# Retention's values in two chunks of 512 columns, with the rotary key's 64 columns as matmuls of their own

## The chip, the core and the metric

The kernel runs on one core of a Trainium2 chip. The metric is the device time of one execution in microseconds. Three runs of the kernel before gave 816.58, 816.60 and 817.53 us; their median, 816.6 us, is the time to which the changed kernel is compared.

## What is computed

The reference is a trunk of two layers over 256 tokens of 2048 features, in float32. The first layer has a combined input projection, two groups of heads (retention and latent attention), a gate and an output projection; the second is a gated convolution module. What matters here is the input projection of the first layer:

```python
h = rms_norm(x, norm_g)
proj = h @ w_in
rq, rk, rv, cq, ckv, krope, gate = jnp.split(proj, list(SPLIT_A), axis=-1)
rv = rv.reshape(B, S, N_RET_HEADS, RET_HEAD_DIM)
k_rope = jnp.broadcast_to(krope[:, :, None, :], (B, S, N_MLA_HEADS, MLA_ROPE_DIM))
```

`rv`, the values of retention, is 1024 columns wide (8 heads of 128), and `krope`, the rotary part of the attention key that all heads share, is 64 columns wide. Both are the same input multiplied by different columns of one weight matrix, over a contraction of 2048.

## The kernel before

**Split products.** Every large product is made of three float32r matmuls (`mm3`, lines 193 to 195): an operand is split into a high part, rounded to float32r, and a low part, the remainder; high times high, high times low and low times high are summed in PSUM. Each of the three instructions loads its own stationary operand (128x128) into the array, also where two that follow one another have the same one.

**The weight stream.** Weights come from HBM through a class `Stream`, in units of 128 partitions by 2048 columns as a rule. A unit is loaded into a buffer `raw` (three of them) by a DMA on SP's queue (line 152). Each half of a unit is then split: ScalarE writes the high part `whi` (line 167, five buffers), and VectorE subtracts it to give the low part `wlo` (line 88 through the helper `tt`, four buffers). When the program asks for half j, the low parts up to half j+3 and the high parts up to half j+4 are issued first (`half`, lines 180 to 186), so that TensorE has some halves in hand. The order of the instructions on TensorE, ScalarE and VectorE is the order in which the program issues them.

**The clock of the program.** Each call of `half` also moves a program clock on to the next whole number and issues the small steps that are due by then (`tick`, `later`). `tick(True)` moves it by one half in between. So what ScalarE and VectorE do beside the weight stream is bound to the count of halves, not to time.

**The stages around the change.** First come the latents for the query (`kgroup`, with 256 tokens as moving columns) and for key and value (two calls of `pair`, also 256 moving columns). Then comes the stage of the values, lines 503 to 520: four chunks `c` of 272 columns, which are the 1024 columns of `rv` and the 64 of `krope` set side by side (1088 in all). Here the input is the stationary operand, 128 tokens at a time (`t` is 0 or 1), and the weights are the moving one. A chunk is 16 steps `k` of the contraction, by 2 token blocks, by the three matmuls of `mm3`: 96 matmuls of 272 columns. The four chunks are 384 of them, and use 8 units of 2176 columns, thus 16 halves of 1088 columns, of which each feeds 24 matmuls. Each chunk fills two PSUM banks (`mmps`, a ring of four) that ScalarE reads out with the norm's scale `Rt` into `vret` (line 518); the last chunk's columns 208 to 271 go to `krope` (line 520).

**What hangs on the stage.** While it runs, VectorE and ScalarE also normalise the latents and make the angles of the rotary embedding, bound to the program clock; TensorE makes two small sums over partitions for that (`token_cols`, line 315). Right behind the stage stand the squares and the rotation of `krope` on ScalarE and VectorE (lines 522 to 529), and then the heads, each with a `pair` (256 moving columns). From the heads on, `chunk` (lines 365 to 382) makes products with 512 moving columns: 16 steps by 2 token blocks by 3, that is 96 matmuls.

Of the kernel before, what the change touches and what calls it, by code (L numbers as in the profile page):

```python
# [10 lines left out]
AF = mybir.ActivationFunctionType  # L11
# [4 lines left out]
P = 128  # L16
T = 256
D = 2048
KT = D // P
# [3 lines left out]
ROPE = 64  # L23
# [3 lines left out]
RVC = 272  # L27
# [21 lines left out]
def body(ctx, tc, a):  # L49
    nc = tc.nc  # L50
    act = nc.scalar.activation
    V = nc.vector
# [12 lines left out]
    def nm(s):  # L65
        uid[0] += 1
        return f"{s}_{uid[0]}"

    def slot(i, dt=F32):
        return spool.tile([P, 2048], dt, tag=f"s{i}", name=nm(f"s{i}"))  # L70
# [7 lines left out]
    def mmps():  # L78
        return psm.tile([P, 512], F32, tag="mm", name=nm("mm"))
# [108 lines left out]
    st = Stream()  # L188

    def mm3(ps, l, r, start, stop):  # L190
        (lh, ll), (rh, rl) = l, r
        mm = nc.tensor.matmul
        mm(ps, lh, rh, start=start, stop=False, skip_group_check=True)  # L193
        mm(ps, lh, rl, start=False, stop=False, skip_group_check=True)  # L194
        mm(ps, ll, rh, start=False, stop=stop, skip_group_check=True)  # L195
# [17 lines left out]

    u_cq = [st.add(a["w_first"][u], V) for u in range(8)]
    u_ckv = [st.add(a["w_in"][i], V) for i in range(4)]
    u_rv = [[st.add(a["w_rv"][2 * c + h], V) for h in range(2)] for c in range(4)]
    u_qk, u_b = {}, {}
    for h in range(HEADS):
        u_qk[h] = [st.add(a["w_in"][4 + 2 * h + i], V) for i in range(2)]
# [28 lines left out]
    def kk(tiles, k):  # L248
        return tiles[k // 8][:, (k % 8) * T:(k % 8 + 1) * T]
# [6 lines left out]
    def consts(what):  # L256
        if what == 0:
            nc.sync.dma_start(posi[:, 0:T + 2], a["pos"])
            nc.sync.dma_start(cb[:, 0:CB_1], a["cb"][:, 0:CB_1])
        elif what == 1:  # L260
            nc.sync.dma_start(dmask[:, :], a["dmask"])
        elif what == 2:
            nc.sync.dma_start(ident[:, :], a["ident"])
            nc.sync.dma_start(amask[:, :], a["amask"])
        else:
            nc.sync.dma_start(cb[:, CB_1:CB_N], a["cb"][:, CB_1:CB_N])
# [8 lines left out]
    for q in range(1, 8):  # L275
        st.before[u_cq[q]] = [lambda q=q: x_load(q)]
    st.before[u_ckv[0]] = [lambda: consts(0)]
    st.before[u_rv[2][0]] = [lambda: consts(1)]
    st.before[u_rv[3][0]] = [lambda: consts(2)]
    st.before[u_rv[3][1]] = [lambda: consts(3)]  # L280

    def x_split(q):
        st.dma_to(q)
# [10 lines left out]
    Rt = cpool.tile([P, 2], F32, name="Rt")  # L294
# [89 lines left out]
    def xrhs(k):  # L384
        return kk(xh, k), kk(xl, k)
# [6 lines left out]
    krope = e0[:, 1024:1152].rearrange("p (t d) -> p t d", t=2)  # L392
# [108 lines left out]
    latent(ckv, 1)  # L501

    vret = slot(9)
    for c in range(4):
        pst = [mmps(), mmps()]
        for uh in range(2):
            for h in range(2):
                hi, lo = st.half(u_rv[c][uh], h)
                for i in range(4):
                    k = uh * 8 + h * 4 + i  # L510
                    w = slice(i * RVC, (i + 1) * RVC)
                    rh, rl = xrhs(k)
                    for t in range(2):
                        tk = slice(t * P, (t + 1) * P)
                        mm3(pst[t][:, :RVC], (rh[:, tk], rl[:, tk]), (hi[:, w], lo[:, w]), k == 0, k == KT - 1)
        for t in range(2):
            n = RVC if c < 3 else 208
            act(vret[:, t * 1024 + c * RVC:t * 1024 + c * RVC + n], pst[t][:, 0:n], AF.Copy, scale=Rt[:, t:t + 1])
            if c == 3:
                act(krope[:, t, :], pst[t][:, 208:272], AF.Copy, scale=Rt[:, t:t + 1])  # L520

    ksq = cpool.tile([P, 2], F32, name="ksq")
    for t in range(2):
# [164 lines left out]
    for h in range(HEADS):  # L688
        m1 = ret_rope(h, pair(u_qk[h], xrhs))
        later(4, lambda h=h, m1=m1: ret_scores(h, m1))  # L690
        if h < 3:
            pst = bproj(u_b[h], 0)
# [5 lines left out]
        elif h < 7:  # L698
            pst = bproj(u_b[h], 1024)
# [113 lines left out]
    for j in range(8):  # L813
        o = (j % 4) * 512
        ps = pair(u_gate[2 * j:2 * j + 2], xrhs)
# [49 lines left out]
    for c in range(4):  # L865
        ps = chunk(u_out[4 * c:4 * c + 4], mrhs)
# [286 lines left out]
    for c in range(4):  # L1153
        ps = chunk(u_cg[4 * c:4 * c + 4], yrhs)
# [26 lines left out]
    for k in range(KT):  # L1181
        hi, lo = st.half(u_co1[k // 2], k % 2)
        l = zrhs(k)
        for t in range(2):
            for c in range(2):
                w = slice(c * 512, (c + 1) * 512)
# [5 lines left out]
    for c in range(2):  # L1192
        us = u_co2[4 * c:4 * c + 4]
        if c == 0:
            ps = chunk(us, zrhs)
# [6 lines left out]
def layout(i):  # L1202
    import numpy as np
    f = np.float32
    A = lambda n: np.asarray(i[n])
    o = {}

    def feat(v):
        return v.reshape(-1, P).T

    def duo(w):
        k, n = w.shape
        return np.ascontiguousarray(w.reshape(2, k // P // 2, P, n // 256, 256).transpose(3, 0, 2, 1, 4)).reshape(n // P, P, -1)

    def kmaj(w, nk):
        k, n = w.shape
        return np.ascontiguousarray(w.reshape(k // P // nk, nk, P, n).transpose(0, 2, 1, 3)).reshape(k // P // nk, P, nk * n)

    def chunks(w, c):
        k, n = w.shape  # L1220
        return np.ascontiguousarray(w.reshape(k // P, P, n // c, c).transpose(2, 1, 0, 3))

    def wide(w):
        k, n = w.shape
        return np.ascontiguousarray(w.reshape(4, 4, P, n // 512, 512).transpose(3, 0, 2, 1, 4)).reshape(n // 128, P, 2048)

    x = A("x")[0]
    o["xt"] = x.reshape(2, P, D).transpose(1, 0, 2).reshape(P, -1)
    o["x"] = np.ascontiguousarray(x.T.reshape(KT, P, T).transpose(1, 0, 2)).reshape(P, -1)
    pos = A("positions")[0]  # L1230
    o["pos"] = np.concatenate([np.broadcast_to(pos[None, :], (P, T)), pos.reshape(2, P).T], 1)
    w = A("a_w_in")[0]
    rq, rk, rv, cq, ckv, kr, gate = np.split(w, [1024, 2048, 3072, 3584, 4096, 4160], axis=1)
    o["w_first"] = kmaj(cq, 2)
    qk = np.stack([rq.reshape(D, HEADS, P), rk.reshape(D, HEADS, P)], 2).reshape(D, -1)
    o["w_in"] = duo(np.concatenate([ckv, qk, gate], 1))
    o["w_rv"] = chunks(np.concatenate([rv, kr], 1), RVC).reshape(4, P, 2, -1).transpose(0, 2, 1, 3).reshape(8, P, -1)
    qb = A("a_w_q_b")[0].reshape(512, HEADS, QK)
    qb = np.concatenate([qb[:, :, :NOPE].reshape(512, -1), qb[:, :, NOPE:].reshape(512, -1)], 1)
    o["w_qb"] = chunks(qb, 512).reshape(3, P, -1)  # L1240
    kvb = A("a_w_kv_b")[0].reshape(512, HEADS, 2 * P)
    kvb = np.concatenate([kvb[:, :, :P].reshape(512, -1), kvb[:, :, P:].reshape(512, -1)], 1)
    o["w_kvb"] = chunks(kvb, 512).reshape(4, P, -1)
    o["w_out"] = wide(A("a_w_out")[0])
    cw = A("c_w_in")[0]
    ca_, cb_, cg_ = np.split(cw, 3, axis=1)
    ab = np.stack([ca_.reshape(D, 8, T), cb_.reshape(D, 8, T)], 2).reshape(D, -1)
    o["c_in"] = wide(np.concatenate([ab, cg_], 1))
    co = A("c_w_out")[0]
    o["c_out1"] = kmaj(co[:, :1024], 2)  # L1250
    o["c_out2"] = wide(co[:, 1024:])

    def inv(d):
        e = -np.arange(0, d, 2, dtype=f) / f(d)
        return np.power(10000.0, e.astype(np.float64)).astype(f)

    def rows(v):
        return np.broadcast_to(v[None, :], (P, v.shape[0]))

    i128 = inv(P)  # L1260
    sgn = np.concatenate([np.ones(64, f), -np.ones(64, f)])
    o["ca"] = np.concatenate([feat(A("a_norm_g")[0]), np.concatenate([i128, i128])[:, None], sgn[:, None], rows(inv(64))], 1)
    qn, kn = A("a_q_norm_g")[0], A("a_k_norm_g")[0]
    cwt = A("c_conv_w")[0].T.reshape(KT, P, TAPS).transpose(1, 0, 2).reshape(P, -1)
    o["cb"] = np.concatenate([feat(A("a_q_a_norm_g")[0]), feat(A("a_kv_a_norm_g")[0]), feat(A("a_ret_norm_g")[0]),
                              qn[:P, None], kn[:P, None], feat(A("c_norm_g")[0]), feat(A("c_conv_b")[0]),
                              feat(A("c_ln_g")[0]), feat(A("c_ln_b")[0]), rows(qn[P:]), rows(kn[P:]), cwt], 1)
    o["ident"] = np.eye(P, dtype=f)
    tri = np.where(np.arange(P)[None, :] <= np.arange(P)[:, None], 0.0, -1e30).astype(f)
    o["amask"] = np.concatenate([np.zeros((P, P), f), tri], 1)  # L1270
    lg = np.log1p(-(2.0 ** (-5.0 - np.arange(HEADS))))
    rel = (np.arange(T)[None, :] - np.arange(P)[:, None]).astype(np.float64)
    dm = np.where(rel >= 0, np.exp(lg[:, None, None] * np.maximum(rel, 0.0)[None]), 0.0) * P ** -0.5
    o["dmask"] = dm.transpose(1, 0, 2).reshape(P, -1).astype(f)
    return {k: np.ascontiguousarray(v) for k, v in o.items()}
# [22 lines left out]
```

## Time and profile before

| what | value |
|---|---|
| median of 3 runs | 816.6 us (816.58 to 817.53) |
| the profiled execution's own time | 816.11 us |
| its span in the trace | 814.3 us |
| instructions in the span | 12383 |
| TensorE matmul busy | 808.1 us (99%) |
| TensorE weight load busy | 720.7 us (89%) |
| VectorE busy | 594.8 us (73%) |
| ScalarE busy | 434.4 us (53%) |
| GpSimd busy | 221.8 us (27%) |
| granted TensorE clock | 1.0 |

The span is the time between the first and the last instruction that the profiler recorded, and the profiled execution took 1.8 us more than that. Busy times are shares of the span by engine. In the profile PE is TensorE's matmul, PEld its weight load, which runs beside it, DVE is VectorE, ACT is ScalarE and SP the engine that issues the DMAs. The recorded duration of one matmul is longer than the distance to the next, since matmuls are pipelined and their ends are modelled; what a matmul costs in a stream is the distance from its start to the next one's. A line such as `mm<-whi,s` names the output and the inputs by the program's names, `x96` is a count, and a bracket at the end of a row of the timeline is the idle time of the engine before that row with what ended it.

### The profile page before, as it was taken

The numbers are of one execution on the slowest core, as the hardware profiler recorded it, in microseconds if no ns is written. First come the engines' busy times: TensorE is split into PE (matmuls) and PEld (weight loads), VectorE is DVE, ScalarE is ACT, GpSimd is POOL, SyncE is SP. The second block draws the span as 40 slices with busy tenths as digits, with TensorE's granted clock in tenths as the row PEclk, the third lists the DMA queues.
The fourth block names the chain that finished last, engine by engine and source line by source line (L and its number), as shares of the span: only waits on it lengthen the run. The fifth ranks groups of instructions, "written<-read, shape, count | busy, mean of one in ns | idle before, by whom it ended". The sixth has DMA issues, their size and how long they took to land.

```text
span 814.3 us, 12383 instructions
## 1 busy us (share of the span) xinstructions
PE 808.1 (99%) x4766; PEld 720.7 (89%) x4766; DVE 594.8 (73%) x1093; ACT 434.4 (53%) x621; POOL 221.8 (27%) x127
## 2 busy tenths in 40 slices
PE   8999999999999999999999999999999999999998
PEld 8999999999999999998888888888888888888886
DVE  5878565699668755575555519999999999698542
ACT  6766544537445654664455644555544565676431
POOL 0000000000000000000000088899999999400000
PEclk9999999999999999999999999999999999999999
DMA  8974545526444443555545455455554554455650
GB/s 280 344 254 166 182 156 196 192 97 213 157 155 148 164 156 111 199 208 207 207 165 197 177 185 200 166 181 206 182 203 162 203 204 163 160 214 194 252 184 26
DMA packets 24106, 150.93 MB, mean 185 GB/s; under 512 B 2800, under 2 KB 3952, under 8 KB 6896
## 3 DMA queue, kind: packets, MB, share of 16 engines
q1 hardware_dynamic: 23616, 148.03, 51.0%
q0 software_dynamic: 288, 2.10, 0.6%
q8 instruction: 37, 0.61, 0.3%
q14 instruction: 21, 0.17, 0.1%
q10 hardware_dynamic: 144, 0.03, 0.0%
HBM read 148.04 MB, written 2.10 MB: 184 GB/s over the span
## 4 chain that ended last, share of the span: by engine, by line
PE 95%; DVE 2%; DMA 1%; ACT 1%; issue 0%; SPq 0%; DVEq 0%; ACTq 0%
PE mm L195 28%; PE mm L193 28%; PE mm L194 28%; PE aux L194 2%; PE aux L193 2%; PE aux L195 2%; DMA raw<-in_w_first 1%; DVE wlo L88 1%; DVE s L88 0%; PE mm L1108 0%; PE aux L853 0%; PE mm L1142 0%; PE aux L661 0%; PE aux L759 0%; PE aux L727 0%; PE aux L728 0%
## 5 line engine op out<-in xcount | busy, mean ns | idle before, releaser
L167 ACT ACTIVATE whi<-raw 128x1024 fp32r<-128x1024 f32 (+2 forms) x278 | 286.8, 1038 | 267.4 <-PE mm L195 177.3
L88 DVE TENSOR_TENSOR wlo<-raw,whi 128x1024 fp32r<-128x1024 f32 (+2 forms) x194 | 228.2, 1185 | 105.9 <-PE mm L194 51.8
L193 PE MATMUL mm<-whi,s 128*128 128x512 f32 (+1 forms) x760 | 285.2, 375 | 0.0
L195 PE MATMUL mm<-whi,s 128*128 128x512 f32 (+1 forms) x760 | 283.1, 372 | 0.0
L194 PE MATMUL mm<-wlo,s 128*128 128x512 f32 (+1 forms) x760 | 283.0, 372 | 0.0
L88 POOL TENSOR_TENSOR wlo<-raw,whi 128x1024 fp32r<-128x1024 f32 x84 | 201.5, 2411 | 33.6 <-PE mm L194 19.2
L91 DVE SCALAR_TENSOR_TENSOR aux<-s,cb,aux 128x256 f32<-128x256 f32 x480 | 190.0, 488 | 12.6 <-ACT aux L904 12.6
L193 PE MATMUL mm<-s,whi 128*128 128x256 f32 x636 | 183.4, 288 | 0.8 <-ACT whi L167 0.8
L195 PE MATMUL mm<-s,wlo 128*128 128x256 f32 x636 | 180.3, 284 | 0.6 <-DVE wlo L88 0.6
L194 PE MATMUL mm<-s,whi 128*128 128x256 f32 x636 | 179.8, 283 | 0.0
L195 PEld LDWEIGHTS mm<-whi,s 128*128 128x128 f32 x760 | 142.7, 188 | 25.0
L193 PEld LDWEIGHTS mm<-whi,s 128*128 128x128 f32 x760 | 142.9, 188 | 23.7
L194 PEld LDWEIGHTS mm<-wlo,s 128*128 128x128 f32 x760 | 142.8, 188 | 23.7
L193 PEld LDWEIGHTS mm<-s,whi 128*128 128x128 f32 x636 | 121.8, 192 | 1.6 <-ACT whi L167 1.0
L195 PEld LDWEIGHTS mm<-s,wlo 128*128 128x128 f32 x636 | 121.8, 191 | 1.4 <-DVE wlo L88 1.2
L194 PEld LDWEIGHTS mm<-s,whi 128*128 128x128 f32 x636 | 121.9, 192 | 0.6
L711 POOL MEMSET s<- 64x256 f32 x8 | 2.9, 361 | 232.3 <-PE mm L195 162.7
L890 POOL MEMSET s<- 128x30 f32 x16 | 1.1, 121 | 116.8 <-PE mm L194 101.0
L791 POOL DMA_DIRECT2D s<-in_xt x2 | 1.2, 618 | 97.2 <-PE aux L728 96.8
L193 PE MATMUL aux<-whi,s 128*128 128x512 f32 x64 | 25.0, 390 | 0.0
L195 PE MATMUL aux<-whi,s 128*128 128x512 f32 x64 | 24.9, 389 | 0.0
L194 PE MATMUL aux<-wlo,s 128*128 128x512 f32 x64 | 24.9, 389 | 0.0
(186 smaller groups left out, 550.1 us busy)
## 6 DMA issues: line engine op xcount, KB each, us to landing
raw<-in_c_in SPq DMA_DIRECT2D x48, 1024.0 KB, 4.8
raw<-in_w_in SPq DMA_DIRECT2D x36, 1024.0 KB, 4.8
raw<-in_w_out SPq DMA_DIRECT2D x16, 1024.0 KB, 4.8
raw<-in_c_out SPq DMA_DIRECT2D x16, 1024.0 KB, 4.8
raw<-in_w_rv SPq DMA_DIRECT2D x8, 1088.0 KB, 5.0
raw<-in_w_kvb SPq DMA_DIRECT2D x4, 1024.0 KB, 4.8
raw<-in_w_first SPq DMA_DIRECT2D x7, 512.0 KB, 4.9
raw<-in_w_qb SPq DMA_DIRECT2D x3, 1024.0 KB, 4.8
```

Of the source, the lines that this page charges most:

```text
L88: (eng or V).tensor_tensor(out=out, in0=in0, in1=in1, op=op)
L91: V.scalar_tensor_tensor(out=out, in0=in0, scalar=s, in1=in1, op0=op0, op1=op1)
L167: act(hi[:, :], self.raw[u][:, h * n:(h + 1) * n], AF.Copy)
L193: mm(ps, lh, rh, start=start, stop=False, skip_group_check=True)
L194: mm(ps, lh, rl, start=False, stop=False, skip_group_check=True)
L195: mm(ps, ll, rh, start=False, stop=stop, skip_group_check=True)
L711: G.memset(krz(i)[64 * b:64 * b + 64, :], 0.0)
L791: G.dma_start(x1[i][:, :], a["xt"][:, i * 2048:(i + 1) * 2048])
L890: G.memset(upad(c, 0, TAPS - 1), 0.0)
```

## The change

The columns of `rv` and of `krope` are no longer set side by side. `rv` is made by two calls of `chunk`, with 512 moving columns each: 192 matmuls of 512 columns instead of 384 of 272. `krope` becomes a product of its own: for 16 steps and 2 token blocks three matmuls with 64 moving columns, 96 in all, into one PSUM bank. The moving columns that pass through TensorE are the same in sum, 104448. The count of matmuls, each with its weight load, goes from 384 to 288. The unit of weights that is loaded for `krope` has 1024 columns, so its two halves have 512 columns and feed 48 matmuls each; the units of `rv` have 2048 columns, and their halves of 1024 feed 12 matmuls each. The stream gets one more unit (9 in place of 8), and the program clock advances by two more. The three loads of constants that stood ahead of the fifth, seventh and eighth unit of the stage stand ahead of the same ones. The readout by ScalarE is four instructions of 512 columns and two of 64, in place of six of 272, two of 208 and two of 64.

```diff
-    u_rv = [[st.add(a["w_rv"][2 * c + h], V) for h in range(2)] for c in range(4)]
+    u_rv = [[st.add(a["w_rv"][4 * c + h], V) for h in range(4)] for c in range(2)]
+    u_kr = st.add(a["w_kr"], V)
...
-    st.before[u_rv[2][0]] = [lambda: consts(1)]
-    st.before[u_rv[3][0]] = [lambda: consts(2)]
-    st.before[u_rv[3][1]] = [lambda: consts(3)]
+    st.before[u_rv[1][0]] = [lambda: consts(1)]
+    st.before[u_rv[1][2]] = [lambda: consts(2)]
+    st.before[u_rv[1][3]] = [lambda: consts(3)]
...
     vret = slot(9)
-    for c in range(4):
-        pst = [mmps(), mmps()]
-        for uh in range(2):
-            for h in range(2):
-                hi, lo = st.half(u_rv[c][uh], h)
-                for i in range(4):
-                    k = uh * 8 + h * 4 + i
-                    w = slice(i * RVC, (i + 1) * RVC)
-                    rh, rl = xrhs(k)
-                    for t in range(2):
-                        tk = slice(t * P, (t + 1) * P)
-                        mm3(pst[t][:, :RVC], (rh[:, tk], rl[:, tk]), (hi[:, w], lo[:, w]), k == 0, k == KT - 1)
+    for c in range(2):
+        ps = chunk(u_rv[c], xrhs)
         for t in range(2):
-            n = RVC if c < 3 else 208
-            act(vret[:, t * 1024 + c * RVC:t * 1024 + c * RVC + n], pst[t][:, 0:n], AF.Copy, scale=Rt[:, t:t + 1])
-            if c == 3:
-                act(krope[:, t, :], pst[t][:, 208:272], AF.Copy, scale=Rt[:, t:t + 1])
+            act(vret[:, t * 1024 + c * 512:t * 1024 + (c + 1) * 512], ps[t][:, :], AF.Copy, scale=Rt[:, t:t + 1])
+    kps = mmps()
+    for k in range(KT):
+        if k % 8 == 0:
+            hi, lo = st.half(u_kr, k // 8)
+        w = slice((k % 8) * ROPE, (k % 8 + 1) * ROPE)
+        for t in range(2):
+            mm3(kps[:, t * ROPE:(t + 1) * ROPE], half_of(xrhs(k), t), (hi[:, w], lo[:, w]), k == 0 and t == 0, k == KT - 1)
+    for t in range(2):
+        act(krope[:, t, :], kps[:, t * ROPE:(t + 1) * ROPE], AF.Copy, scale=Rt[:, t:t + 1])
```

**Where it moves instructions on TensorE.** The place is the end of the stage of the values and the first product of the heads. In the kernel before, `mm_1188` is the second PSUM bank of the fourth chunk, `mm_1329` the bank of the first head, `whi` and `wlo` are the split weights, and `s_5` to `s_8` the split input:

```order
L193 MATMUL mm_1188<-whi_1159,s_6_102 128x272
L194 MATMUL mm_1188<-wlo_1189,s_6_102 128x272
L195 MATMUL mm_1188<-whi_1159,s_8_104 128x272
L193 MATMUL mm_1329<-s_5_101,whi_1193 128x256
L194 MATMUL mm_1329<-s_7_103,whi_1193 128x256
L195 MATMUL mm_1329<-s_5_101,wlo_1219 128x256
```

In the changed kernel `mm_954` is the second bank of the second chunk, `mm_1107` the bank of `krope`:

```order
L193 MATMUL mm_954<-whi_1023,s_6_102 128x512
L194 MATMUL mm_954<-wlo_1037,s_6_102 128x512
L195 MATMUL mm_954<-whi_1023,s_8_104 128x512
L193 MATMUL mm_1107<-whi_1041,s_5_101 128x64
L194 MATMUL mm_1107<-wlo_1055,s_5_101 128x64
L195 MATMUL mm_1107<-whi_1041,s_7_103 128x64
```

Between the last product of the values and the first of the heads there now stand 96 matmuls of 64 columns, in groups of three as everywhere.

**Where it moves instructions on ScalarE.** The place is the same seam. In the kernel before, `mm_1187` and `mm_1188` are the fourth chunk's banks, `s_106` is `vret`, `e_107` is `krope`, and the `whi` behind them is the fifth half of the heads' weights:

```order
L518 ACTIVATE s_106_747<-mm_1187,Rt 128x208
L520 ACTIVATE e_107<-mm_1187,Rt 128x64
L518 ACTIVATE s_106_747<-mm_1188,Rt 128x208
L520 ACTIVATE e_107<-mm_1188,Rt 128x64
L525 ACTIVATE t_1310,ksq<-e_107 128x64
L525 ACTIVATE t_1316,ksq<-e_107 128x64
L167 ACTIVATE whi_1334<-raw_1191 128x1024
```

In the changed kernel `mm_953` and `mm_954` are the second chunk's banks and `mm_1107` that of `krope`:

```order
L508 ACTIVATE s_106_747<-mm_953,Rt 128x512
L508 ACTIVATE s_106_747<-mm_954,Rt 128x512
L167 ACTIVATE whi_1112<-raw_1039 128x1024
L167 ACTIVATE whi_1164<-raw_1039 128x1024
L517 ACTIVATE e_107<-mm_1107,Rt 128x64 x2
L522 ACTIVATE t_1217,ksq<-e_107 128x64
L522 ACTIVATE t_1223,ksq<-e_107 128x64
L167 ACTIVATE whi_1241<-raw_1073 128x1024
```

The readout of the values and that of `krope`, which followed one another, are now two stops of ScalarE with two halves of the heads' weights between them.

More of the change, by code (lines that the diff above doesn't have):

```diff
@@ L1236, in layout @@
     o["w_in"] = duo(np.concatenate([ckv, qk, gate], 1))
-    o["w_rv"] = chunks(np.concatenate([rv, kr], 1), RVC).reshape(4, P, 2, -1).transpose(0, 2, 1, 3).reshape(8, P, -1)
+    o["w_rv"] = wide(rv)
+    o["w_kr"] = kr.reshape(KT, P, ROPE).transpose(1, 0, 2).reshape(P, -1)
     qb = A("a_w_q_b")[0].reshape(512, HEADS, QK)
```

## The prediction

> **What bounds the kernel now.** I read the page first, for the engine that is busy and the chain that ended last, and then the waits. The page's busy line and its chain by engine:
>
> ```profile
> PE 808.1 (99%) x4766; PEld 720.7 (89%) x4766; DVE 594.8 (73%) x1093; ACT 434.4 (53%) x621; POOL 221.8 (27%) x127
> PE 95%; DVE 2%; DMA 1%; ACT 1%; issue 0%; SPq 0%; DVEq 0%; ACTq 0%
> ```
>
> TensorE is the bound, and by nearly all of the span. The waits of its weight loads and of its matmuls on VectorE and ScalarE are the rows that would show a second bound:
>
> ```profile
> PEld mm L195 <- DVE wlo L88: 1.2, 3, 0.6
> PE mm L193 <- ACT whi L167: 0.8, 1, 0.8
> ```
>
> In 814 us it waits about 2 us for split weights. So what TensorE gets more or less to do in a stage moves the end by as much, and what the other engines are spared is worth nothing. The stretches, from the windows (the columns are span, then PE, PEld, DVE, ACT and POOL busy with counts, the granted clock, the DMA share and GB/s), are the stage of the values, the heads and gate, and the rest:
>
> ```profile
> 54.60:103.56 48.96, 48.96 (x395) 48.96 (x393) 33.55 (x63) 27.54 (x38) 1.66 (x4) 1.00 0.54 189
> 103.56:362.52 258.96, 258.61 (x1947) 249.03 (x1945) 180.85 (x293) 137.89 (x215) 2.92 (x13) 1.00 0.46 165
> 362.52:812.00 449.48, 447.95 (x2024) 371.02 (x2022) 340.46 (x674) 230.43 (x306) 216.82 (x105) 1.00 0.51 184
> ```
>
> In the stage of the change TensorE has no gap at all, its granted clock is 1.00, and there is one weight load for every matmul. No later stage has idle time of TensorE in which a delay could be made good: 0.35 us in the second stretch, 1.5 us in the third.
>
> **What the stage costs now.** The matmuls of the stage in order of time (start, modelled duration, engine, line, operation), at its begin, around the two small sums, and at its end:
>
> ```profile
> 54.60 0.29 PE L193 MATMUL mm<-whi,s 128*128 128x272 f32 x1
> ...
> 60.50 0.29 PE L195 MATMUL mm<-whi,s 128*128 128x272 f32 x1
> 60.63 0.50 PE L315 MATMUL aux<-ones,t 128*128 128x1 f32 x4
> 60.99 0.37 PE L193 MATMUL mm<-whi,s 128*128 128x272 f32 x1
> 61.20 0.29 PE L194 MATMUL mm<-wlo,s 128*128 128x272 f32 x1
> ...
> 72.97 0.29 PE L195 MATMUL mm<-whi,s 128*128 128x272 f32 x1
> 73.10 0.50 PE L315 MATMUL aux<-ones,t 128*128 128x1 f32 x4
> 73.46 0.37 PE L193 MATMUL mm<-whi,s 128*128 128x272 f32 x1
> 73.67 0.29 PE L194 MATMUL mm<-wlo,s 128*128 128x272 f32 x1
> ...
> 103.44 0.28 PE L195 MATMUL mm<-whi,s 128*128 128x272 f32 x1
> 103.56 0.28 PE L193 MATMUL mm<-s,whi 128*128 128x256 f32 x1
> ```
>
> Between 60.50 and 61.20 lie two matmuls of 272 columns and a small sum, which the trace has as four instructions of one column. Two halves of 24 matmuls lie ahead of the first sum, so from 54.60 to 60.50 are 47 steps, 0.1255 us each; from 61.20 to 72.97, the 50th to the 144th, are 94 of 0.1252. So the four take 0.70 - 2 x 0.125 = 0.45 us; the other sum, from 72.97 to 73.67, gives the same 0.45. The products then take 48.96 - 2 x 0.45 = 48.06 us, which is 48.06 / 384 = 0.1252 us each.
>
> **What 512 columns cost.** The same operation with 512 columns runs in the output projection, with the weights as moving operand as here; its second matmul of a chunk, and the transposes behind the chunk's last:
>
> ```profile
> 386.79 0.39 PE L194 MATMUL mm<-wlo,s 128*128 128x512 f32 x1
> ...
> 408.32 1.03 PE L853 MATMUL aux<-ident,s 128*128 128x128 f32 x8
> ```
>
> A chunk has 96 matmuls, so 95 lie between: (408.32 - 386.79) / 95 = 0.2266 us; with the somewhat longer first one of a chunk I take 0.227. The two chunks of values cost 192 x 0.227 = 43.6 us.
>
> From 272 to 512 columns the price rises by (0.2266 - 0.1252) / 240 = 0.00042 us a column; what is left at no columns is about 0.011 us. Wide matmuls thus pay by the column with a small constant, and 96 fewer instructions alone would be worth about a microsecond. The whole question is whether that line holds down to 64 columns.
>
> **What 64 columns cost.** The trace has no float32r matmul under 256 columns. One lower bound is that line: 0.1252 - 208 x 0.00042 = 0.037 us. But each of these matmuls also needs a stationary operand of 128 columns, and the small sums show what a load costs that no stream covers. The loads around the first of them:
>
> ```profile
> 60.51 0.54 PEld L315 LDWEIGHTS aux<-ones,t 128*128 128x128 f32 x4
> 60.97 0.19 PEld L193 LDWEIGHTS mm<-whi,s 128*128 128x128 f32 x1
> 61.08 0.19 PEld L194 LDWEIGHTS mm<-wlo,s 128*128 128x128 f32 x1
> ```
>
> Four loads for four matmuls of a single column take (60.97 - 60.51) / 4 = 0.115 us each, and the 0.45 us above say 0.1125 each. The column streamed there is next to nothing, so this is the load's own price; and the two loads behind them, which belong to the float32r products and follow without cover, stand 0.11 apart. The matmuls' own starts, 60.63 to 60.99, give 0.09 each, but the 272 behind them starts its successor late, so 0.09 is only a second lower bound. The upper neighbour is the 256-column matmul, which cannot be cheaper than one of 64:
>
> ```profile
> 359.76 0.28 PE L194 MATMUL mm<-s,whi 128*128 128x256 f32 x1
> ...
> 362.52 0.40 PE L193 MATMUL mm<-whi,s 128*128 128x512 f32 x1
> ```
>
> From the first row to the next operation are 23 of them: 2.76 / 23 = 0.120 us. A stream of 256 or 272 columns is about as long as a load, which is why the load never showed in this kernel. I take 0.1125 us, the row nearest in kind (a full load, hardly any stream): 96 x 0.1125 = 10.8 us.
>
> Of the Trainium skill, "TensorE: Matmul & The Clock Gate", section Back-to-back issue gap, speaks against this: its formula for a warm matmul is the columns over 2.4 GHz and 2.5 ns, an estimated 29 ns for 64 columns. By that formula the 96 would cost 2.8 us, and the sum below would be 43.6 + 2.8 - 48.1 = -1.7 us, a gain. The same section warns that the formula leaves the load out at small widths, and gives 81 ns as measured for 128 columns in a real stream; by that the 96 would cost at most 7.8 us, and the sum be +3.3. The single-column rows of this trace agree with neither figure: they took 112 ns.
>
> **The sum.** On the path: out go 48.06 us, in come 43.6 + 10.8 = 54.4 us; the two small sums stay. That is +6.3 us. The profiled execution took 816.11 us, 0.5 below the median of 816.6; I add the difference to the median: **822.9 us**. With 0.10 us (the 0.11 between two rows, less their rounding) to 0.120 a matmul it is +5.1 to +7.1; with 0.09 it is +4.2.
>
> **What else moves, at no cost.** The splits: sixteen pieces of 1088 become sixteen of 1024 and two of 512, and each of the first sixteen now lasts TensorE 12 x 0.227 = 2.72 us instead of 24 x 0.125 = 3.0. So the feeding engines have to be 9% faster over the two chunks. The closest place is where they are fullest; VectorE's splits of the eleventh to the thirteenth piece of the stage:
>
> ```profile
> 77.65 1.28 DVE L88 TENSOR_TENSOR wlo<-raw,whi 128x1088 fp32r<-128x1088 f32 x1
> 78.86 0.32 DVE L468 TENSOR_SCALAR s<-s 128x320 f32<-128x320 f32 x1
> 79.21 0.49 DVE L85 TENSOR_SCALAR s<-s 128x640 f32<-128x640 f32 x1
> 79.71 1.29 DVE L88 TENSOR_TENSOR wlo<-raw,whi 128x1088 fp32r<-128x1088 f32 x1
> 83.70 1.29 DVE L88 TENSOR_TENSOR wlo<-raw,whi 128x1088 fp32r<-128x1088 f32 x1 [2.70 <-ACT whi L167]
> ```
>
> The last of these, the thirteenth piece, is done at 84.99, after a wait for ScalarE, which had the sine to make. TensorE needs it after twelve pieces: now at 54.60 + 36.0 + 0.9 = 91.5, then at 54.60 + 32.7 + 0.9 = 88.2. Even if nothing before it came earlier, 3.2 us would be in hand. The loads of a unit land well inside that:
>
> ```profile
> DMA to landing us min/median/max: 4.6/5.0/6.4
> ```
>
> That is the answer for `raw` in this stretch; a buffer is asked for again when its second half has been split, three halves ahead of TensorE, and its new contents are split four halves ahead, so about four halves (10.9 us) lie between. At the seam, VectorE and ScalarE stop for `krope` until TensorE is through:
>
> ```profile
> 104.06 0.43 DVE L88 TENSOR_TENSOR t<-e 128x64 f32<-128x64 f32 x3 [2.14 <-ACT e L520]
> ...
> 105.27 1.22 DVE L88 TENSOR_TENSOR wlo<-raw,whi 128x1024 fp32r<-128x1024 f32 x1
> ```
>
> Behind that wait stands the split of the heads' fourth half, done at 106.49, 2.9 us after the stage's end at 103.56. TensorE has three halves of the heads in hand by then, 72 x 0.120 = 8.6 us. This stays so: the wait for `krope` grows to the length of the last 48 small matmuls, but the same three halves are split ahead of it. If that cover were gone, the heads would start up to 2.9 us late. ScalarE's shorter readout and the smaller splits spare engines that wait anyway, and count as nothing.
>
> **The rivals.**
>
> *The stream hides the loads after all* (5%, the other side). If loads overlapped each other, or the second of two equal operands were not loaded, 64 columns would cost as the line says, 0.037 us: 3.6 us, a sum of -0.9, and 815.7 us. For it speaks that wide matmuls hide their loads completely; against it the single-column rows. It is also what the formula of the Trainium skill above amounts to. It decides at (48.06 - 43.6) / 96 = 0.046 us: below that the change is no loss.
>
> *Load and stream add up* (6%). The load is hidden by the matmul ahead of it; if a stream as short as this cannot run while the next load does, the price is 0.1125 + 63 x 0.00042 = 0.139 us, 13.3 us in all, +8.9, and 825.5 us. Against it: in the 256-column stream load and stream overlap, or 0.120 would be above 0.2. "TensorE: Matmul & The Clock Gate" of the Trainium skill (Part 3, The mechanism) says that a load overlaps a matmul in flight only if it goes to another group of rows. Full loads like these would then never be hidden; the 0.120 us of the 256s disagree.
>
> *Small matmuls run at a worse rate* (5%). At the kernel's start the 256-column matmuls were slow:
>
> ```profile
> 4.86 1.90 PE L343 MATMUL mm<-s,whi 128*128 128x256 f32 x8
> 6.60 0.64 PE L346 MATMUL mm<-s,wlo 128*128 128x256 f32 x4
> ```
>
> Eight of them took 1.74 us, 0.2175 each instead of 0.120, though TensorE was busy since 1.00. If a stretch of thin matmuls brings that pace back, or the narrow form goes at half rate for another reason, 96 cost twice 0.1125: 21.6 us, +17.1, and 833.7 us.
>
> *The faster pace starves TensorE* (4%). If splits come late in the chunks, or at the seam, by half of the 2.9 us that stand there, the sum is +7.8 and the time 824.4 us.
>
> **How the numbers follow.** The forecast has 80%. The range goes from 820.8, which is the forecast with 0.09 us a matmul (+4.2), to 825.5, where load and stream add up; it takes in the starving as well, and leaves out the hidden loads and the worse rate, 10%, beside what no case here names. A measurement of this kernel can tell about 0.2%, 1.6 us, from no change. Slower by more needs over (48.06 + 1.6 - 43.6) / 96 = 0.063 us a matmul: all cases but the first rival, and I give 94%. Of that rival's part, and what lies between, 4% falls within the bound, and 2% on a gain, for which the small matmuls would have to cost under (48.06 - 1.6 - 43.6) / 96 = 0.030 us.
>
> **What would show it.** In the profile after, the 512s of the stage should stand 0.227 us apart, the 64s 0.11, with a weight load in front of each and no idle time named; the stage should last 55.3 us (54.4 and 0.9), and everything behind it should be as long as before. The forecast is wrong if the 64s stand under 0.06 or over 0.13 us apart, or if the rows show TensorE waiting for `whi`, `wlo` or a PSUM bank in or just behind the stage; and its reason is wrong if the stage lengthens as forecast but through such waits.

## The result and the profile after

The changed kernel takes 830.34 us, the median of four runs (828.91 to 830.88). The kernel before, run beside it, takes 817.07 (816.58 to 818.48). The ratio is 1.0164, with a 95% interval from 1.0152 to 1.0176: 12.4 to 14.4 us slower. The forecast was 822.9 us, in a range from 820.8 to 825.5, and the measured time lies above it; the sign was right, and the loss of 13.3 us is twice what was forecast.

The page of the profiled execution (830.21 us, span 828.4) first, by its busy line, the chain by engine and the row of the granted clock in 40 slices:

```profile
PE 822.7 (99%) x4670; PEld 727.7 (88%) x4670; DVE 594.7 (72%) x1095; ACT 433.4 (52%) x619; POOL 221.5 (27%) x127
PE 96%; DVE 2%; DMA 1%; ACT 1%; issue 0%; SPq 0%; DVEq 0%; ACTq 0%
PEclk9999969999999999999999999999999999999999
```

In the kernel before, the row of the clock was

```profile
PEclk9999999999999999999999999999999999999999
```

TensorE is as busy as before, and still the whole chain. New is one digit: in the sixth slice (103.5 to 124.2 us) the granted clock is not full. The waits of TensorE answer the forecast's question whether the splits would starve it:

```profile
PEld mm L195 <- DVE wlo L88: 1.6, 4, 0.5
PE mm L193 <- ACT whi L167: 0.2, 1, 0.2
```

They do not; these are the same small waits as before. The stretches of the stage and behind it (columns as in the prediction; the granted clock stands behind POOL's count):

```profile
54.51:99.05 44.54, 44.54 (x203) 36.94 (x201) 31.46 (x64) 25.30 (x34) 1.57 (x4) 1.00 0.53 192
99.05:102.09 3.04, 3.04 (x29) 3.04 (x28) 1.23 (x1) 1.83 (x3) 0.00 (x0) 1.00 0.30 43
102.09:116.58 14.49, 14.49 (x70) 14.49 (x70) 1.23 (x1) 1.06 (x1) 0.00 (x0) 0.50 0.15 63
116.58:119.25 2.67, 2.67 (x13) 2.67 (x14) 2.03 (x9) 1.93 (x7) 0.00 (x0) 0.51 0.00 0
119.25:828.40 709.15, 705.09 (x3956) 618.64 (x3954) 519.42 (x958) 365.11 (x512) 219.52 (x118) 1.00 0.49 177
```

The first row is the two chunks of 512 columns. The second and third are the 96 matmuls of 64 columns: 3.04 us at full clock, then 14.49 us at half. The fourth is the begin of the first head, still at half clock; then the clock is back. TensorE is busy in every microsecond of the four. The matmuls at the three seams, in order of time:

```profile
99.05 0.19 PE L193 MATMUL mm<-whi,s 128*128 128x64 f32 x1
99.08 0.28 PE L194 MATMUL mm<-wlo,s 128*128 128x64 f32 x1
99.19 0.28 PE L195 MATMUL mm<-whi,s 128*128 128x64 f32 x1
...
101.98 0.28 PE L193 MATMUL mm<-whi,s 128*128 128x64 f32 x1
102.09 0.39 PE L194 MATMUL mm<-wlo,s 128*128 128x64 f32 x1
102.29 0.40 PE L195 MATMUL mm<-whi,s 128*128 128x64 f32 x1
102.50 0.40 PE L193 MATMUL mm<-whi,s 128*128 128x64 f32 x1
...
116.37 0.40 PE L195 MATMUL mm<-whi,s 128*128 128x64 f32 x1
116.58 0.56 PE L193 MATMUL mm<-s,whi 128*128 128x256 f32 x1
...
119.25 0.28 PE L193 MATMUL mm<-s,whi 128*128 128x256 f32 x1
119.37 0.28 PE L194 MATMUL mm<-s,whi 128*128 128x256 f32 x1
```

From 99.08 to 101.98 the 64s stand 0.111 us apart (26 steps in 2.90 us). From 102.50 to 116.37 they stand 13.87 / 65 = 0.213 apart. Twelve of the 256s need 2.67 us instead of 12 x 0.120 = 1.44.

**Where the 14.1 us of the two spans went** (828.4 against 814.3). The stage starts 0.1 earlier. It lasts 116.58 - 54.51 = 62.07 us instead of 48.96, that is +13.1: -4.4 by the chunks (44.54, in which the two small sums are 0.9) and +17.5 by the key's product. Behind it come +1.2 us in the first head. The rest is as long as before, within 0.2 us.

### The profile page after: what moved, and what is told of

Same layout as the page of the kernel before. It is cut to its first block, busy times and chain, and to the rows that moved or that the text cites. A ratio compares the mean times of both kernels' runs of the same rounds, so it can differ in the third digit from the quotient of the medians.

```text
span 828.4 us, 12197 instructions
## 1 busy us (share of the span) xinstructions
PE 822.7 (99%) x4670; PEld 727.7 (88%) x4670; DVE 594.7 (72%) x1095; ACT 433.4 (52%) x619; POOL 221.5 (27%) x127
## 4 chain that ended last, share of the span: by engine, by line
PE 96%; DVE 2%; DMA 1%; ACT 1%; issue 0%; SPq 0%; DVEq 0%; ACTq 0%
PE mm L195 28%; PE mm L193 28%; PE mm L194 28%; PE aux L195 2%; PE aux L193 2%; PE aux L194 2%; DMA raw<-in_w_first 1%; DVE wlo L88 1%; DVE s L88 0%; PE mm L1105 0%; PE aux L850 0%; PE mm L1139 0%; PE aux L658 0%; PE aux L756 0%; PE aux L724 0%; PE aux L725 0%
## 5 line engine op out<-in xcount | busy, mean ns | idle before, releaser
L167 ACT ACTIVATE whi<-raw 128x1024 fp32r<-128x1024 f32 (+1 forms) x280 | 286.6, 1031 | 278.1 <-PE mm L195 184.6
L88 DVE TENSOR_TENSOR wlo<-raw,whi 128x1024 fp32r<-128x1024 f32 (+1 forms) x196 | 228.7, 1175 | 115.1 <-PE mm L194 55.8
L195 PEld LDWEIGHTS mm<-whi,s 128*128 128x128 f32 x728 | 140.0, 192 | 27.5
L194 PEld LDWEIGHTS mm<-wlo,s 128*128 128x128 f32 x728 | 140.1, 192 | 26.2
L193 PEld LDWEIGHTS mm<-whi,s 128*128 128x128 f32 x728 | 140.0, 192 | 26.1
```

The lines of the kernel that those rows point to most:

```text
L88: (eng or V).tensor_tensor(out=out, in0=in0, in1=in1, op=op)
L167: act(hi[:, :], self.raw[u][:, h * n:(h + 1) * n], AF.Copy)
```

## The experiments

Theory A: the granted clock follows how much TensorE streams, that is, for what share of the time moving columns pass through it. At the 0.00042 us a column of the prediction a matmul of 64 columns streams for 0.027 us and one of 512 for 0.213, and the weight load makes the former last 0.111, so a stretch of them streams 0.24 of the time; kept up for about 3 us, that loses the clock. Theory B: the half rate belongs to the narrow form itself or to the number of such matmuls or loads in a row, whatever stands around them. The experiments change what stands around the 64s, or their width. Since the stage starts anywhere from 54.5 to 56.8 us in these traces, stages are compared by their own length.

**The key's product in bursts of 12.** Its weights get tiles of their own, so that its matmuls can stand anywhere:

```diff
+    plan = {i + 9: (2 * i, 2 * i + 1) for i in range(8)}
     for c in range(2):
-        ps = chunk(u_rv[c], xrhs)
+        if c == 1:
+            kr_split()
+        ps = chunk(u_rv[c], xrhs, None, lambda i, c=c: kr_steps(plan.get(8 * c + i, ())))
...
+    kr_steps(plan.get(16, ()))
```

`kr_steps(ks)` issues six matmuls of 64 columns for each step k of its list, ahead of the half i of a chunk.

> The key's 96 matmuls of 64 columns come in eight bursts of 12, each behind a half of the second chunk of values (12 matmuls of 512 columns). Theory A (the clock is halved because a stretch of thin matmuls streams too little: in the changed kernel 27 ns of streaming in each 111 ns, a share of 0.24): the share over a burst and a half is (12 x 0.027 + 12 x 0.213) / 4.05 = 0.71, the clock stays at 1.0, each of the 96 costs 0.111 us, the stage lasts 43.6 + 10.7 + 0.9 = 55.2 us, the time is 817.1 + 6.3 = 823.4. Theory B (matmuls of this narrow form come to half rate by their own number or form, whatever stands around them): the half rate of 0.213 us is seen again after some 27 of them, the time is 830 or more.

Measured: 827.56 us, ratio 1.0128 (1.0113 to 1.0143). That lies between the theories, and the rows say why. The first burst and the wide matmuls behind it (`aux` is the key's bank here, the second `s` the tile with its weights):

```profile
80.91 0.39 PE L195 MATMUL mm<-whi,s 128*128 128x512 f32 x1
82.57 0.30 PE L193 MATMUL aux<-s,s 128*128 128x64 f32 x1 [1.28 <-ACT s L512]
83.83 0.30 PE L194 MATMUL aux<-s,s 128*128 128x64 f32 x1 [0.96 <-DVE s L88]
...
85.08 0.40 PE L195 MATMUL aux<-s,s 128*128 128x64 f32 x1
85.29 0.77 PE L193 MATMUL mm<-whi,s 128*128 128x512 f32 x1
85.86 0.63 PE L194 MATMUL mm<-wlo,s 128*128 128x512 f32 x1
```

In this kernel the split of the key's weights came so late that TensorE stood still for 2.24 us, and behind that the clock fell, so that seven matmuls of 512 columns ran slow. The other seven bursts ran at full clock. One of the four runs kept a mean clock of 1.000 (0.998 in the others) and took 826.22 us, so most of the excess is the stop itself. The run speaks for theory A, but only the kernel without the stop, below, is clean.

**In bursts of 24:**

```diff
-    plan = {i + 9: (2 * i, 2 * i + 1) for i in range(8)}
+    plan = {2 * i + 10: range(4 * i, 4 * i + 4) for i in range(4)}
```

> As the kernel with bursts of 12, but four bursts of 24 (2.67 us each at 0.111), each behind two halves of the second chunk (5.4 us). In the changed kernel the clock fell 3.0 us after the thin stretch began. Theory A with a mean over about that long: bursts of 2.67 us are just too short, clock 1.0, 823.4 us; if it looks over less, or over fixed stretches that a burst can fill most of, the clock falls in some bursts and the wide matmuls behind them run slow for a while: 824 to 830. Theory B: 830 or more.

Measured: 822.98 us, ratio 1.0075 (1.0060 to 1.0090). The stage in one row:

```profile
54.72:109.97 55.25, 55.25 (x299) 47.57 (x297) 33.34 (x63) 27.86 (x36) 1.56 (x4) 1.00 0.44 160
```

The clock is 1.00 throughout, and the stage lasts 55.25 us where the prediction had 55.3. The same 96 matmuls, the same loads, the same narrow form: without the loss of the clock the change costs about what was forecast. That the narrow form brings the half rate by itself is ruled out. A limit on the number in a row is not yet: a burst has 24, and the changed kernel ran 28 before the clock fell. The fillers and the 128 columns, below, decide that.

**The block again, as a control for those tiles**, `plan = {16: range(16)}`:

> Control for the kernels with bursts: the key's weights are split into tiles of their own ahead of the second chunk, as there, but all 96 matmuls stand in one block behind the second chunk, as in the changed kernel. Theories A and B: as the changed kernel, 0.111 us each for 3 us, then 0.213 at half clock, 830.3 us within 1.

Measured: 831.97 us, ratio 1.0186 (1.0165 to 1.0208). The 96 matmuls:

```profile
99.94:117.69 17.75, 17.75 (x98) 17.75 (x96) 0.00 (x0) 0.88 (x2) 0.00 (x0) 0.58 0.00 0
```

17.75 us at a mean clock of 0.58. The tiles are not what helped the bursts. The two runs, 830.97 and 832.97 us, lie 1.7 us above the forecast on average, more than the 1 it allowed; in the profiled one, part of that arises behind the stretch, as is shown further down.

**The chunks without the key.** The loop of 64 columns goes, and `krope` is copied from `ps[t][:, 0:ROPE]`.

> The two chunks of 512 columns alone: the product for the key is left out, and the key is copied from the last chunk's first columns, so this part of the work is not done. Theories A and B: 48.06 us of products become 43.6, clock 1.0 throughout, 817.1 - 4.5 = 812.6 us. If the chunks of 512 carry some of the loss (waits for splits or banks), the time is above 814.

Measured: 812.30 us, ratio 0.9944 (0.9929 to 0.9959).

```profile
55.31:99.84 44.53, 44.53 (x202) 36.93 (x201) 32.33 (x62) 26.15 (x34) 1.33 (x4) 1.00 0.55 198
```

44.53 us, that is 43.6 and the two sums. The half of the change that was meant to gain shortens the stage by its 4.4 us; nothing of the loss is in the chunks.

**More work to keep the clock.**

```diff
+    spare = auxps()
     for k in range(KT):
...
         for t in range(2):
             mm3(kps[:, t * ROPE:(t + 1) * ROPE], half_of(xrhs(k), t), (hi[:, w], lo[:, w]), k == 0 and t == 0, k == KT - 1)
+        nc.tensor.matmul(spare[:, :], half_of(xrhs(k), 1)[0], hi[:, 0:512], start=True, stop=True)
```

> The changed kernel with work added: behind every six matmuls of the key one matmul of 512 columns into a bank that nobody reads, 16 in all. Theory A: the share of streaming in the stretch is (6 x 0.027 + 0.213) / 0.89 = 0.42; if that is enough to keep the clock, the stretch lasts 16 x 0.89 = 14.3 us instead of 17.5 and the 1.2 us lost behind it go too: 830.3 - 4.4 = 825.9, faster with more work. If 0.42 is not enough, the clock still falls: 834 to 837. Theory B: the half rate stays, and the added matmuls come on top, 834 or more.

Measured: 826.50 us, ratio 1.0117 (1.0100 to 1.0134). The stretch of the key:

```profile
101.01:115.41 14.40, 14.40 (x113) 13.71 (x112) 2.45 (x2) 3.00 (x5) 0.00 (x0) 1.00 0.21 74
```

With 16 useless matmuls on top it lasts 14.40 us at full clock, in place of 17.53, mostly at half. The kernel gets about 4 us faster by doing more, as theory A alone expects.

**How little is enough.** The same with a filler only behind every second or every fourth step, `if k % 2 == 1` and `if k % 4 == 3` ahead of the added line:

> The changed kernel with one unused matmul of 512 columns behind every twelve of the key, 8 in all: the share of streaming in the stretch is (12 x 0.027 + 0.213) / (12 x 0.111 + 0.227) = 0.34. Theory A with a limit under 0.34: clock 1.0, the stretch lasts 8 x 1.56 = 12.5 us instead of 17.5, nothing is lost behind it: 830.3 - 6.3 = 824.0 us. Theory A with a limit between 0.34 and the 0.42 that was enough: the clock falls after 3 us, 831 to 833.

> The same with one unused matmul of 512 columns behind every 24 of the key, 4 in all: share (24 x 0.027 + 0.213) / (24 x 0.111 + 0.227) = 0.30. Theory A with a limit under 0.30: clock 1.0, 4 x 2.89 = 11.6 us, 830.3 - 7.2 = 823.1 us. With a limit above: the clock falls, 830 to 832. If the clock looks at fixed stretches of about 3 us, bursts of 24 in a row with a single wide matmul may also lose it in some of them: between the two.

Measured: 834.57 us, ratio 1.0211 (1.0189 to 1.0233), with eight fillers, and 832.50 us, ratio 1.0185 (1.0144 to 1.0227), with four. The stretch with eight, up to where the clock falls and behind it:

```profile
99.71:105.67 5.96, 5.96 (x52) 5.83 (x51) 1.23 (x1) 1.83 (x3) 0.00 (x0) 1.00 0.49 176
105.67:118.00 12.33, 12.33 (x55) 11.91 (x55) 1.23 (x1) 1.34 (x3) 0.00 (x0) 0.51 0.00 0
```

and with four:

```profile
101.31:104.47 3.16, 3.16 (x29) 3.12 (x28) 1.23 (x1) 1.83 (x3) 0.00 (x0) 1.00 0.29 47
104.47:118.00 13.53, 13.53 (x64) 13.34 (x63) 1.23 (x1) 1.06 (x1) 0.00 (x0) 0.50 0.16 67
```

Both lose the clock, after 6.0 and 3.2 us. With eight the kernel pays for the fillers besides, and takes longer than the 831 to 833 us expected. With four the runs spread from 829.31 to 835.09 us, at mean clocks of 0.992 and 0.985, and can't be told from those of the changed kernel. So a share of 0.34 is too little and 0.42 was enough. It is not the length of a run of thin matmuls: runs of 12 lost the clock here, with one wide matmul between them, and runs of 24 kept it where 5.4 us of wide ones lay between.

How long the half clock lasts is read off from its fall to its return, in the changed kernel, the control block, with eight and with four fillers, and in the first bursts of 12:

```profile
102.13:119.20 17.07, 17.07 (x82) 17.07 (x82) 3.20 (x10) 2.99 (x8) 0.00 (x0) 0.50 0.13 54
102.76:123.24 20.48, 20.48 (x98) 20.48 (x98) 2.36 (x9) 2.19 (x8) 0.00 (x0) 0.50 0.07 20
105.83:122.89 17.06, 17.06 (x77) 16.58 (x77) 3.57 (x10) 2.99 (x8) 0.00 (x0) 0.50 0.07 22
104.52:125.00 20.48, 20.48 (x95) 20.19 (x95) 3.58 (x10) 2.99 (x8) 0.00 (x0) 0.50 0.15 53
84.88:88.29 3.41, 3.41 (x11) 2.83 (x11) 1.17 (x2) 0.00 (x0) 0.00 (x0) 0.50 0.63 221
```

These are 5, 6, 5, 6 and 1 times 3.413 us (20.48 / 6). So in these traces the clock changes on a grid of fixed steps of 3.413 us, and where a stretch lies on the grid is a matter of chance that bears on how long it keeps the clock and on how much is lost behind it. The control's first head got the clock back only after 26 matmuls, which took 5.64 us instead of 3.12; it lost 2.5 us there, and the changed kernel 1.2. If the mean over one step is what counts, which no run shows, the limit can be estimated more closely. The control's last step ahead of the fall, 99.35 to 102.76, has 0.59 us of 512s, which stream 0.213 of 0.227, and 2.82 us of 64s: a share of 0.36, too little. A burst of 24 fills at most 2.67 us of a step, so no step of that kernel streams less than 0.39, and that was enough.

**128 columns at the same pace of loads.** High and low part of the key's weights stand side by side in `kw`:

```diff
-            mm3(kps[:, t * ROPE:(t + 1) * ROPE], half_of(xrhs(k), t), (hi[:, w], lo[:, w]), k == 0 and t == 0, k == KT - 1)
+            for i in range(2):
+                nc.tensor.matmul(kps[:, t * P:(t + 1) * P], half_of(xrhs(k), t)[i], kw[:, k * P:(k + 1) * P], start=k == 0 and t == 0 and i == 0, stop=k == KT - 1 and i == 1, skip_group_check=True)
```

> The high and low parts of the key's weights side by side as one moving operand: 64 matmuls of 128 columns in place of 96 of 64, the two halves of the result added on VectorE (the product of the two low parts comes in with it). The load still sets the pace: 0.111 us. Theory A: the share of streaming is 0.053 / 0.111 = 0.48. If that keeps the clock: 64 x 0.111 = 7.1 us, 43.6 + 7.1 - 48.06 = +2.6, 819.7 us. If not: 27 x 0.111 + 37 x 0.213 + 1.2 = 12.1 us, 824.7. Theory B, in which the narrow form matters: as the latter.

Measured: 820.22 us, ratio 1.0041 (1.0027 to 1.0055). The 64 matmuls:

```profile
100.47:107.56 7.09, 7.09 (x65) 7.09 (x64) 0.00 (x0) 0.89 (x2) 0.00 (x0) 1.00 0.01 5
```

0.111 us each over 7.09 us, with a load for each, at clock 1.00. The load sets the pace of 64 and of 128 columns alike; only the share of streaming differs, 0.24 against 0.48, and only the former loses the clock. Nor is it the number in a row: 64 matmuls with 64 loads kept the clock here, and the changed kernel lost it after 28. With that, theory B falls in both forms.

**The bursts of 12 without the stop:** `kr_split()` is not called at the begin of the second chunk, but by `later(4, kr_split)`, four halves into the first.

> The bursts of 12 again, with the key's weights split four halves into the first chunk instead of at the begin of the second. In the first try TensorE stood still for 2.2 us in the first burst, since the split came too late, and the clock fell behind that. Theory A (the clock follows the share of streaming): without that stop all eight bursts run at 0.111 us with the clock at 1.0, the stage lasts 55.2 us, 823.4 us. Theory B (thin matmuls bring the half rate even in bursts of 12): the clock falls as before and the time stays at 827.

Measured: 823.01 us, ratio 1.0077 (1.0059 to 1.0096).

```profile
54.80:110.16 55.36, 55.36 (x299) 47.58 (x297) 33.23 (x63) 27.77 (x36) 1.23 (x4) 1.00 0.44 160
```

Clock 1.00 and 55.36 us, as theory A had it; what the first try lost more was its own late split, and the clock lost behind that.

**Two ways without narrow matmuls.** The key's weights as stationary operand:

```diff
-    for k in range(KT):
-        if k % 8 == 0:
-            hi, lo = st.half(u_kr, k // 8)
...
+    for k in range(KT):
+        for i in range(2):
+            nc.tensor.matmul(kps[:, 0:T], kw[:, k * P:(k + 1) * P], xrhs(k)[i], start=k == 0 and i == 0, stop=k == KT - 1 and i == 1)
```

> Roles swapped for the key: its weights, high and low part side by side, are the stationary operand of 128 columns, and all 256 tokens of the input move: 32 matmuls of 256 columns at 0.120 us = 3.8 us, and two transposes (0.2 us) a little later. Theories A and B: clock 1.0, 43.6 + 3.8 + 0.2 - 48.06 = -0.4, 816.7 us, no difference that can be told from the kernel before.

Measured: 816.11 us, ratio 0.9995 (0.9986 to 1.0004). The key's product, 32 matmuls up to the first head:

```profile
101.26 4.00 PE L519 MATMUL mm<-s,s 128*128 128x256 f32 x32
105.09 0.28 PE L193 MATMUL mm<-s,whi 128*128 128x256 f32 x1
```

3.83 us in place of 17.53. The product comes out transposed; it is turned back and rotated a little later, beside the first head. And three equal chunks, from the kernel before (each chunk also takes its weights in four units, so there are 24 pieces of 728 columns, and every second one moves the program clock on by a half only):

```diff
-RVC = 272
+RVC = 364
...
-    for c in range(4):
+    for c in range(3):
```

> Values and key side by side as in the kernel before, but in three chunks of 364 columns (four of the 1092 are zeros that are not used): 288 matmuls of 364 columns. By the line through 272 and 512 columns one costs 0.1252 + 92 x 0.00042 = 0.164 us, 47.2 us in all, clock 1.0: -0.9, 816.2 us. That is what 96 fewer instructions are worth where none is narrower than a load.

Measured: 816.65 us, ratio 0.9999 (0.9990 to 1.0008).

```profile
55.16:103.91 48.75, 48.75 (x298) 48.75 (x297) 35.82 (x70) 29.87 (x44) 1.46 (x4) 1.00 0.58 197
```

48.75 us, 0.2 less than before and not the 0.9 expected: (48.75 - 0.9) / 288 = 0.166 us a matmul, a little over the line. Both versions take less time than the changed kernel, and neither can be told from the kernel before.

## Why the prediction was wrong, step by step

- **TensorE as the only bound: right.** The delay of the stage comes through to the end in full, and the waits did not grow.
- **The chunks of 512: right.** 43.6 us were forecast; 44.54 and 44.53 with the two sums were measured.
- **The price of 64 columns, "96 x 0.1125 = 10.8 us": the step that failed.** The price itself was right, 0.111 us, and so was its reason, a load that no stream covers. It was taken as constant over a stretch of 10.8 us. The granted clock of 1.00 was read in the stage before and carried over without a reason, so that the sum has no term for the clock. The price held for 3.04 us; the other 68 cost 0.213 each, which is past the 0.13 that the forecast gave as its own sign of being wrong. That is 17.53 - 10.8 = 6.7 us, and with the 1.2 us in the first head, less the 0.1 by which the stage started earlier, it is (rounded) the 7.8 us between the forecast +6.3 and the measured +14.1 of the spans. With the clock kept, the bursts show the sum as it was meant: 822.98 and 823.01 us.
- **The rival with the worse rate: right in kind, wrong in size and chance.** It had 5% and the whole stretch at half rate, 833.7 us. It does not mention the clock. The row quoted for it, 256 columns in 0.2175 us at the kernel's start, has the pace of the half clock, and should have led to the question what holds the clock. That it was the clock is not shown, since the profile gives 1.00 there; but the same eight matmuls took 1.80 us in the changed kernel and 1.06 with the roles swapped, so their pace is not a matter of their form. I judged TensorE by being busy, 99%; the share that it streams is 64 columns' worth out of some 0.11 us, and could have been worked out beforehand. The limit that this share has to keep could not: no row of the kernel before shows it.
- **The other rivals.** Loads were not hidden (0.111, not 0.037). Load and stream did not add up either: 64 and 128 columns cost the same 0.111. Nothing starved.
- **The figures of the Trainium skill** ("TensorE: Matmul & The Clock Gate", Back-to-back issue gap), an estimated 29 ns for 64 columns by its formula, and 81 ns for 128: the 64s measured 111 ns and the 128s too, with this operation and a load for each. The statement of the Trainium skill ("TensorE: Matmul & The Clock Gate", Part 3, The mechanism) that a load overlaps a matmul in flight only in another group of rows: the 0.120 us of the 256s, and the equal price of 64 and 128, are against it. That section of the Trainium skill also lets a load run ahead into a background buffer, and with that these figures agree.

What the Trainium skill says of the gate ("TensorE: Matmul & The Clock Gate", Part 1, What's actually happening) agrees with most of this: the clock has a full and a half rate, a block sets it by how busy the array was of late, over windows of some 3.4 us. Here the clock was 1.00 or 0.50, fell 3.0, 3.2 and 6.0 us into thin stretches, and lay at half for whole multiples of 3.413 us. The advice of the Trainium skill for keeping the clock ("TensorE: Matmul & The Clock Gate", Why this matters for your kernels) is to leave no idle gap of over about 3 us; in the changed kernel there was no gap at all, and the clock fell.

Open stays where between 0.34 and 0.42 the limit lies (between 0.36 and 0.39 by the estimate over one step), and whether it is the stream that is counted or something that goes with it, such as the columns that reach PSUM.

## What to carry to other kernels

Before narrowing a matmul's moving operand, divide its streaming time by what it will really last: here a load of 128 columns sets 0.111 us, so going under 256 columns, at 0.120 us, saves next to nothing, and a stretch that streams 0.34 or less of its time for a few microseconds also loses the clock, for itself and for what follows. If such matmuls can't be avoided, spread them among wide ones (822.98 us against 830.34), make them wider at the same price (820.22), or swap the operands so that the narrow side is the stationary one (816.11). A busy share of 99% says nothing about that; look at the granted clock by stretches.

## What I had not expected of the hardware

TensorE can lose half its clock while it has an instruction in hand at every moment, when it mostly loads weights: 28 loads and 28 matmuls of 64 columns in 3.04 us in the changed kernel. The clock then comes back only on a grid of 3.413 us, so what this costs can differ between runs of one kernel (830.97 and 832.97 us for the control block). And work that nobody needs can pay: 16 matmuls of 512 columns brought the stretch from 17.53 to 14.40 us.
